# One filling block moved from RWKV's second inverse to the HGRN2 stage: half projections there in ten turns, four of them in turns 0 to 3

## The chip, the cores and the metric

The kernel runs on one NeuronCore of one Trainium2 chip. The metric is device time in microseconds (us) for one execution of the whole program, the median of three runs. The tensor engine (PE) multiplies; the vector engine (DVE), the scalar engine (ACT) and GpSimd (POOL) do elementwise work; SP issues most of the DMAs, and ACT and POOL issue some. Each engine takes its instructions in the order in which they were written down for it.

## The reference

One decoder layer over 1024 tokens of width 1024, in fp32. Three groups of heads share one input projection, and a feed-forward block and an embedding gate follow:

```python
z = rmsnorm(h, norm_mix_g) @ w_in            # (1024 x 1024) @ (1024 x 3840)
a_q, a_f, a_i, a_g, b_q, b_k, b_v, c_in = split(z)
o_a = hgrn2_mix(a_q, a_f, a_i, a_g, ...)     # 4 heads, gated linear recurrence
o_b = dilated_window_mix(b_q, b_k, b_v)      # 4 heads, three dilated windows
o_c = rwkv7_mix(c_in, ...)                   # 4 heads, delta rule recurrence
h = h + concat([o_a, o_b, o_c]) @ w_out
h = h + conv_glu_ffn(rmsnorm(h), ...)
h = h + sigmoid(rmsnorm(h) @ w_gate) * (p @ w_p)
return rmsnorm(h)
```

## The kernel before

`w_in` is cut into 30 blocks of 128 output columns, numbered 0 to 29. A block's projection is 8 row tiles times 2 token halves times 3 products: each operand is split into a rounded part and a remainder (`whi`, `wlo`, `xh`, `xl`), and `mm3` multiplies hi by hi (line 130), hi by lo (132) and lo by hi (134). That makes 48 matmuls of 128x512 for a block and 24 for one half of it. Blocks 0 to 7 feed RWKV directly. The other 22 (8 to 23 for HGRN2: f, q, i, g of each head; 24 to 29 for attention: q, k, v of two head pairs) are finished (scaled by the norm factor `R`; a sigmoid on f, q and g; q and g multiplied by the input of the sigmoid as well) and stored in DRAM as `z8` to `z29`, and are read back (`zl`) by the stage that uses them. Since PE needs none of RWKV's results for these products, they serve as filling.

`rwkv` treats two pairs of heads, p = 0 and 1, each in four steps. `rwkv_prep` makes the scores and projects one filling block. `rwkv_inverse` inverts unit triangular 32x32 blocks with 62 short DVE instructions (lines 698 and 700), turns the result through DRAM (`Tz`, `Uz`, then `Tc`) and needs no PE; meanwhile `project_rest` puts whole blocks on PE. `rwkv_main` goes through four groups of chunks (`rwkv_groups`), with PE, DVE, ACT and POOL in the order written; `fill` puts three matmuls of a further block between its steps, and `pending("z")` finishes a block at the start of the next group. The rest of those blocks follows with the output norm. The list `FILL` holds the number of blocks for each of these places, and the order of the blocks is fixed:

```python
js = iter((*range(8, 16), 24, 25, 26, 16, 17, 18, 20, 21, 22, 27, 28, 29, 19, 23))
...
self.project_rest([next(js) for _ in range(self.FILL[2 * p] - 1)])
...
steps = self.project_steps([next(js) for _ in range(self.FILL[2 * p + 1])])
...
self.rest = list(js)
```

Whatever is left then is projected in the HGRN2 stage, one half per turn, by `project_late` (tile `zp`). That stage interleaves four streams by an order that is written out for 38 turns: A (heads 0 and 2 of HGRN2), B (heads 1 and 3, from turn 6), C (attention, in the turns of `TURNS`) and F (a half projection, in the turns of `LATE`; its last turn only opens the tiles for the output projection):

```python
for r in range(38):
    order += "C" * (r in self.TURNS) + "A" + "B" * (r > 5) + "F" * (r in self.LATE)
interleave(order, {"A": A, "B": B, "C": self.swa(sp), "F": self.project_late(self.rest)})
```

A head of HGRN2 loads f and q (lines 987 to 992), multiplies the first scores (line 1008, `hsc`), then takes seven levels, one a turn: scores on PE (line 1029), a masked copy (1031) and two updates (1032, 1034) on DVE or POOL. In attention `swq` are scores (1186), 1193 their maximum on DVE, 1195 the exponential on ACT, `swt` transposes (1209) and `swo` values (1222). In this stage a scheduler may move an instruction of one stream past those of another on the same engine; in the four groups of `rwkv_main` it may only bring in work from outside.

Of the kernel before, what the change touches and what calls it, by code (L numbers as in the profile page):

```python
# [67 lines left out]
def interleave(order, streams):  # L68

    live = dict(streams)  # L70
    while live:
        for s in order:
            if s in live and next(live[s], STOP) is STOP:
                del live[s]
# [5 lines left out]
class Trunk:  # L80
# [227 lines left out]
    def phase_mix(self):  # L308
# [8 lines left out]
        with self.pool("hg") as slots, self.pool("sw") as sp:  # L317
# [8 lines left out]
            for r in range(38):  # L326
                order += "C" * (r in self.TURNS) + "A" + "B" * (r > 5) + "F" * (r in self.LATE)
            interleave(order, {"A": A, "B": B, "C": self.swa(sp), "F": self.project_late(self.rest)})

    TURNS = [i * 33 // 22 for i in range(23)]  # L330
    LATE = 0, 1, 4, 7, 9, 11, 13, 15, 17

    def mix_norm(self):

# [182 lines left out]
    def rwkv(self):  # L517
# [7 lines left out]
        for p in (0, 1):  # L525
            d = {}
            with tc.tile_pool(name=f"pre{p}", bufs=1) as tp:
                with tc.manual_schedule(engines={mybir.EngineType.PE}):
                    self.rwkv_prep(p, tp, lt, d, next(js))
                self.rwkv_inverse(p, tp, d)  # L530
            self.project_rest([next(js) for _ in range(self.FILL[2 * p] - 1)])
            E = mybir.EngineType
            self.pend = {}
            steps = self.project_steps([next(js) for _ in range(self.FILL[2 * p + 1])])
            with self.pool(f"rk{p}") as rp:
# [10 lines left out]
            self.rwkv_norm_out(p, sg, d, 1)  # L546
        self.rest = list(js)

    FILL = (6, 3, 6, 3)

    def rwkv_prep(self, p, tp, lt, d, j):

# [1343 lines left out]
```

## Time and profile before

| | |
|---|---|
| median of 3 runs | 1459.96 us (1458.23 to 1460.84) |
| the profiled execution, its own time | 1458.02 us |
| its span, first to last instruction | 1456.2 us |
| granted PE clock, mean of the span | 0.995 |
| PE busy | 1427.3 us, 98% |
| DVE busy | 1102.3 us, 76% |
| ACT busy | 635.3 us, 44% |
| second inverse, with the filling on PE | about 279 to 334 us |
| four groups of the second head pair | about 334 to 404 us |
| HGRN2 and attention stage | about 413 to 617 us |

A row of the timeline reads: start, duration, engine, line, operation, tiles written and read, shape, count; in brackets the time that the engine sat idle just before it and what ended that. A busy PE is one with a matmul in flight: neighbouring matmuls overlap, so that 48 rows of 0.39 us each take 10.9 us together. A row of a table by windows reads: window, its length, then busy time and number of instructions of PE, of PE's weight loads, of DVE, ACT and POOL, then granted clock, DMA share and GB/s.

### The profile page before, as it was taken

The page shows a single profiled execution, that of the slowest core. Times are in us where ns is not written, and L with a number is a line of the kernel's source. Part 1 is how long each engine was busy: PE and PEld are TensorE (multiplying, and loading weights), DVE is VectorE, ACT ScalarE, POOL GpSimd, SP SyncE. Part 2 cuts the span into 40 slices and gives each one's busy share as a digit, 9 for nine tenths or more (in the row PEclk, how much of TensorE's full clock was granted, in tenths as well). Part 3 has the DMA queues.
Part 4 walks back from the last instruction along what each step waited for, and adds up shares of the span by engine and source line. Part 5 has one row for each costly group of instructions (what it writes and reads, how often), then busy time and mean ns, then how long its engine had stood idle before and what let it go on. Part 6 is the DMA issues. An engine that isn't in the chain of part 4 may idle for free.

```text
span 1456.2 us, 20345 instructions
## 1 busy us (share of the span) xinstructions
PE 1427.3 (98%) x7480; PEld 1174.8 (81%) x7480; DVE 1102.3 (76%) x1672; ACT 635.3 (44%) x1131; POOL 447.3 (31%) x364
## 2 busy tenths in 40 slices
PE   9999999999999999899999999999999999999996
PEld 7888887888877777788878888888888888888885
DVE  6567565684677689637798889888888799777685
ACT  6531443213434565335544434444444444455552
POOL 2332342223421132222145545544454000002342
PEclk9999999999999999999999999999999999999998
DMA  5224021240151320165423332333333883352443
GB/s 215 69 82 114 30 74 58 66 129 31 58 203 44 116 73 23 66 224 209 153 93 109 109 100 96 109 103 107 108 96 122 311 287 96 103 165 58 127 157 115
DMA packets 80019, 167.84 MB, mean 115 GB/s; under 512 B 20080, under 2 KB 22256, under 8 KB 79920
## 3 DMA queue, kind: packets, MB, share of 16 engines
q1 hardware_dynamic: 65568, 145.44, 30.2%
q10 hardware_dynamic: 13408, 17.57, 3.6%
q0 software_dynamic: 944, 3.54, 0.7%
q8 instruction: 59, 0.97, 0.3%
q14 instruction: 40, 0.33, 0.1%
HBM read 120.12 MB, written 46.40 MB: 114 GB/s over the span
## 4 chain that ended last, share of the span: by engine, by line
PE 85%; DVE 6%; issue 3%; ACT 2%; POOL 2%; DMA 2%; SPq 0%; DVEq 0%; ACTq 0%; POOLq 0%
PE bg L1351 15%; PE bv L1351 11%; PE dp L130 8%; PE dp L134 8%; PE dp L132 8%; PE bg L1669 7%; PE bv L1669 7%; PE hsc L1029 2%; PE bv L130 1%; PE bv L134 1%; PE bv L132 1%; PE bg L130 1%; PE bg L132 1%; PE bg L134 1%; PE swq L1186 1%
## 5 line engine op out<-in xcount | busy, mean ns | idle before, releaser
L130 PE MATMUL dp<-xh,whi 128*128 128x512 f32 x544 | 197.5, 408 | 1.3 <-ACT xh L375 1.3
L134 PE MATMUL dp<-xh,wlo 128*128 128x512 f32 x544 | 189.1, 393 | 0.1
L132 PE MATMUL dp<-xl,whi 128*128 128x512 f32 x544 | 188.5, 392 | 0.4 <-DVE xl L376 0.3
L108 POOL TENSOR_TENSOR wlo<-raw,whi 128x512 fp32r<-128x512 f32 x84 | 136.4, 1643 | 75.1 <-ACT whi L106 75.1
L108 POOL TENSOR_TENSOR wlo<-wraw,whi 128x512 fp32r<-128x512 f32 x63 | 89.3, 1422 | 226.8 <-ACT whi L106 208.2
L1351 PE MATMUL bg<-t,whi 128*128 128x512 f32 x352 | 132.5, 389 | 0.8 <-DVE ct L1554 0.8
L106 ACT CAST whi<-wraw 128x512 fp32r<-128x512 f32 x120 | 72.6, 617 | 129.8 <-PE dp L132 87.0
L130 PEld LDWEIGHTS dp<-xh,whi 128*128 128x128 f32 x544 | 101.6, 189 | 24.0 <-issue 3.5
L134 PEld LDWEIGHTS dp<-xh,wlo 128*128 128x128 f32 x544 | 102.3, 188 | 22.3 <-POOL wlo L108 0.5
L132 PEld LDWEIGHTS dp<-xl,whi 128*128 128x128 f32 x544 | 102.4, 189 | 20.4 <-DVE xl L376 0.6
L108 POOL TENSOR_TENSOR wlo<-s,whi 128x512 fp32r<-128x512 f32 x44 | 66.6, 1514 | 160.9 <-ACT whi L106 160.9
L1669 PE MATMUL bg<-t,whi 128*128 128x512 f32 x308 | 94.9, 389 | 0.0
L1669 PE MATMUL bv<-t,whi 128*128 128x512 f32 x308 | 94.8, 389 | 0.0
L106 ACT CAST whi<-s 128x512 fp32r<-128x512 f32 x66 | 39.0, 620 | 122.3 <-PE bg L1351 113.4
L106 ACT CAST whi<-raw 128x512 fp32r<-128x512 f32 x88 | 52.7, 619 | 90.9 <-issue 48.3
L175 POOL TENSOR_TENSOR rst<-rst,mhalf 128x4 f32<-128x4 f32 (+1 forms) x9 | 10.1, 1130 | 222.7 <-DVE rst L173 222.7
L108 DVE TENSOR_TENSOR wlo<-wraw,whi 128x512 fp32r<-128x512 f32 x57 | 47.7, 836 | 40.2 <-ACT whi L106 35.8
L1351 PEld LDWEIGHTS bg<-t,whi 128*128 128x128 f32 x352 | 66.0, 188 | 14.7 <-ACT whi L106 1.1
L1665 ACT CAST t<-t 128x512 fp32r<-128x512 f32 x77 | 47.8, 623 | 47.6 <-PE bv L1669 34.1
L1669 PEld LDWEIGHTS bv<-t,whi 128*128 128x128 f32 x308 | 57.8, 188 | 12.0
L1669 PEld LDWEIGHTS bg<-t,whi 128*128 128x128 f32 x308 | 57.7, 188 | 12.0
L1351 PE MATMUL bg<-t,wlo 128*128 128x512 f32 x176 | 67.2, 389 | 0.0
(424 smaller groups left out, 3610.6 us busy)
## 6 DMA issues: line engine op xcount, KB each, us to landing
raw<-in_ffn_up_dram SPq DMA_DIRECT2D x44, 512.0 KB, 3.7
wraw<-in_w_in_dram SPq DMA_DIRECT2D x29, 512.0 KB, 3.7
z<-zst SPq DMA_DIRECT2D x18, 512.0 KB, 2.8
gb<-ct SPq DMA_DIRECT2D x33, 256.0 KB, 2.3
t<-gb SPq DMA_DIRECT2D x33, 256.0 KB, 2.8
t<-gt SPq DMA_DIRECT2D x33, 256.0 KB, 2.7
zl<-z SPq DMA_DIRECT2D x16, 512.0 KB, 4.1
wraw<-in_ple_gate_dram SPq DMA_DIRECT2D x16, 512.0 KB, 3.6
```

The costliest lines, as they stand in the source:

```text
L106: nc.scalar.copy(hi, src)
L108: eng.tensor_tensor(lo, src, hi.bitcast(F32), ALU.subtract)
L130: nc.tensor.matmul(ps[hf], wh, xh[hf], start=first, stop=False)
L132: nc.tensor.matmul(ps[hf], wh, xl[hf], start=False, stop=False)
L134: nc.tensor.matmul(ps[hf], wl, xh[hf], start=False, stop=last)
L175: nc.gpsimd.tensor_tensor(r2[:, :n], r[:, :n], self.mhalf[:, :n], ALU.pow)
L1029: nc.tensor.matmul(sc[:, c, :], ks[:, c * P:(c + 1) * P], view(qt, c * P, [2 * n, 64 // n], [HT + n, 2], [1, n]), start=True, stop=True)
L1186: nc.tensor.matmul(pq[h][:, b:b + w], d["q"][hs, qb * P:nk], d["k"][hs, b:b + w], start=True, stop=True)
L1351: nc.tensor.matmul(ps, w[part == 2][:, s], X[k][part == 1], start=start and k == part == 0, stop=k == 3 and part == 2, skip_group_check=no ...
L1665: nc.scalar.copy(xh, x)
L1669: nc.tensor.matmul(ps[m], wt[part == 2][:, m * P:(m + 1) * P], (xh, xl)[part == 1], start=k == part == 0, stop=k == NK - 1 and part == 2)
```

## The change

```diff
-    LATE = 0, 1, 4, 7, 9, 11, 13, 15, 17
+    LATE = 0, 1, 2, 3, 5, 7, 9, 11, 13, 15, 17
...
-    FILL = (6, 3, 6, 3)
+    FILL = (6, 3, 5, 3)
```

During the second inverse PE now has four whole blocks (26, 16, 17, 18) behind the one of `rwkv_prep` (25). Block 20 goes to the steps of `rwkv_main`, so that these hold 20, 21, 22 and no longer 21, 22, 27. Block 27 goes to the HGRN2 stage, which projects five blocks (27, 28, 29, 19, 23) in ten halves and no longer four in eight. The turns of the halves are 0, 1, 2, 3, 5, 7, 9, 11, 13, 15, where they were 0, 1, 4, 7, 9, 11, 13, 15.

On PE, between the inverse's filling and the first group of the second pair: the end of the filling and the start of the group (`dp` are the projections, `pt` transposes, `py` the first product with the inverse `T`). Before, the last block `dp_2787` (block 20) stands between `dp_2723` (block 18) and the group; of its 48 rows the last six are shown:

```order
L130 MATMUL dp_2787<-xh_119,whi_2783 128x512
L130 MATMUL dp_2787<-xh_103,whi_2783 128x512
L132 MATMUL dp_2787<-xl_120,whi_2783 128x512
L132 MATMUL dp_2787<-xl_104,whi_2783 128x512
L134 MATMUL dp_2787<-xh_119,wlo_2785 128x512
L134 MATMUL dp_2787<-xh_103,wlo_2785 128x512
L821 MATMUL pt_2891<-cst,v_2304 128x128 x2
L130 MATMUL dp_2894<-xh_105,whi_2845 128x512
L132 MATMUL dp_2894<-xl_106,whi_2845 128x512
L134 MATMUL dp_2894<-xh_105,wlo_2847 128x512
L860 MATMUL py_2901<-T_2885,ABt_2877 128x128 x4
```

```order
L132 MATMUL dp_2723<-xl_120,whi_2719 128x512
L132 MATMUL dp_2723<-xl_104,whi_2719 128x512
L134 MATMUL dp_2723<-xh_119,wlo_2721 128x512
L134 MATMUL dp_2723<-xh_103,wlo_2721 128x512
L821 MATMUL pt_2825<-cst,v_2304 128x128 x2
L130 MATMUL dp_2828<-xh_105,whi_2779 128x512
L132 MATMUL dp_2828<-xl_106,whi_2779 128x512
L134 MATMUL dp_2828<-xh_105,wlo_2781 128x512
L860 MATMUL py_2835<-T_2819,ABt_2811 128x128 x4
```

The group follows block 18 at once, and its first filling matmuls are those of block 20.

On DVE, from the end of the third group of the second pair through most of the fourth (`S` are steps of the state, `wlo` a weight's remainder, `X` a copy that the next PE product `pgm` reads). Before:

```order
L940 SCALAR_TENSOR_TENSOR S_3391<-pS_3392,gC_2414,N_3355 128x64
L940 SCALAR_TENSOR_TENSOR S_3398<-pS_3399,gC_2414,N_3355 128x64
L108 TENSOR_TENSOR wlo_3683<-wraw_3675,whi_3681 128x512
L940 SCALAR_TENSOR_TENSOR S_3405<-pS_3406,gC_2414,N_3355 128x64
L794 TENSOR_TENSOR U_3412<-Tc_2510,cst 128x512
L740 TENSOR_TENSOR sc_2307<-sc_2307,gnr_3303 128x512
L785 TENSOR_TENSOR AKt_3449<-sc_3444,pm_2858 128x256
L785 TENSOR_TENSOR W_2865<-sc_3444,pm_2858 64x4x64 x2
L108 TENSOR_TENSOR wlo_3857<-wraw_3853,whi_3855 128x512
L883 COPY_PREDICATED U_3412<-cmask,pu_3456 128x512
L828 COPY pb_2862<-pt_3462 64x2x64 x4
L470 TENSOR_TENSOR zst_3600<-dp_3183,rstd 128x512 x2
```

After:

```order
L108 TENSOR_TENSOR wlo_3616<-wraw_3612,whi_3614 128x512
L940 SCALAR_TENSOR_TENSOR S_3330<-pS_3331,gC_2414,N_3287 128x64
L940 SCALAR_TENSOR_TENSOR S_3337<-pS_3338,gC_2414,N_3287 128x64
L794 TENSOR_TENSOR U_3344<-Tc_2510,cst 128x512
L740 TENSOR_TENSOR sc_2307<-sc_2307,gnr_3235 128x512
L785 TENSOR_TENSOR AKt_3381<-sc_3376,pm_2792 128x256
L785 TENSOR_TENSOR W_2799<-sc_3376,pm_2792 64x4x64 x2
L883 COPY_PREDICATED U_3344<-cmask,pu_3388 128x512
L828 COPY pb_2796<-pt_3394 64x2x64 x4
L306 TENSOR_TENSOR dp_3117<-dp_3117,rstd 128x512
L108 TENSOR_TENSOR wlo_3733<-wraw_3725,whi_3731 128x512
L475 TENSOR_TENSOR zst_3532<-zst_3532,dp_3117 128x512
```

A weight's remainder now stands ahead of the last two steps of the state, where it stood ahead of the last; and the block finished here is 21, a q block with a sigmoid, of which the first half's scaling (306) and product (475) stand ahead of the copy `X`, where two plain scalings (470) of block 22 stood.

On ACT, about turn 15 of the HGRN2 stage (`hV` and `hkt` are the transposed values and keys of head 1, which PE's `hkv` needs; `ob` is attention's output, cast for the output projection). Before:

```order
L473 ACTIVATE zst_4475<-zp_4563 128x512
L1053 COPY hV_4621<-vt_4622 128x512
L1053 COPY hV_4621<-vt_4628 128x512
L1059 COPY hkt_4634<-vt_4635 128x512
L1195 ACT_TABLE_LOAD
L1195 ACTIVATE lg_4607,sden_4602<-lg_4607,sden_4602 128x128
L1195 ACTIVATE lg_4610,sden_4602<-lg_4610,sden_4602 128x128
L1059 COPY hkt_4634<-vt_4641 128x512
L155 CAST xh_4689<-ob_3827 128x512
```

After:

```order
L473 ACTIVATE zst_4478<-zp_4566 128x512
L155 CAST xh_4692<-ob_3830 128x512
L1053 COPY hV_4624<-vt_4625 128x512
L1195 ACT_TABLE_LOAD
L1195 ACTIVATE lg_4610,sden_4605<-lg_4610,sden_4605 128x128
L1195 ACTIVATE lg_4613,sden_4605<-lg_4613,sden_4605 128x128
L1053 COPY hV_4624<-vt_4631 128x512
L1059 COPY hkt_4637<-vt_4638 128x512
L1059 COPY hkt_4637<-vt_4644 128x512
```

The cast of `ob` moved ahead of all four copies, and the table load and two exponentials ahead of three of them.

## The prediction

> **What bounds the kernel now.** I read the page's head first, then a table by windows cut at the stages, then the timeline around the three places that the change touches. Head and table:
>
> ```profile
> span 1456.2 us, 20345 instructions
> PE 1427.3 (98%) x7480; PEld 1174.8 (81%) x7480; DVE 1102.3 (76%) x1672; ACT 635.3 (44%) x1131; POOL 447.3 (31%) x364
> PE 85%; DVE 6%; issue 3%; ACT 2%; POOL 2%; DMA 2%; SPq 0%; DVEq 0%; ACTq 0%; POOLq 0%
> core 0: us, PE busy (x) PEld busy (x) DVE busy (x) ACT busy (x) POOL busy (x), PEclk, DMA share, GB/s
> 279.00:334.30 55.30, 55.30 (x243) 45.37 (x242) 37.79 (x90) 7.19 (x11) 10.97 (x13) 1.00 0.36 106
> 334.30:413.00 78.70, 76.71 (x593) 63.82 (x592) 46.46 (x103) 33.49 (x100) 30.81 (x37) 1.00 0.23 75
> 426.60:440.00 13.40, 13.16 (x79) 10.35 (x78) 13.06 (x30) 5.60 (x17) 4.02 (x5) 1.00 0.31 98
> 440.00:490.00 50.00, 49.76 (x331) 37.86 (x331) 32.55 (x65) 24.93 (x48) 7.91 (x7) 1.00 0.12 38
> 490.00:520.00 30.00, 28.22 (x236) 24.54 (x234) 24.98 (x39) 18.01 (x31) 7.38 (x8) 1.00 0.38 141
> 520.00:545.00 25.00, 22.65 (x169) 17.34 (x165) 20.32 (x51) 17.51 (x42) 9.63 (x8) 1.00 0.29 96
> 545.00:580.00 35.00, 32.78 (x268) 25.49 (x269) 33.61 (x67) 19.74 (x41) 7.58 (x7) 1.00 0.05 16
> 580.00:617.00 37.00, 33.20 (x276) 28.99 (x276) 24.12 (x43) 14.30 (x26) 9.35 (x8) 1.00 0.17 52
> ```
>
> The chain that ended last is 85% PE, and PE is in use for 98% of the span. So a matmul that is moved from one place where PE is full to another costs there what it saves here. Only PE's idle time can be won: 2.0 us in the four groups (78.70 less 76.71), 0.2 at 426 to 440 and 0.2 up to 490, but 1.8, 2.4, 2.2 and 3.8 us in the last four windows, where DVE is busy up to 96% (33.61 of 35). The change puts its products at 427 to 440, ahead of that idle time.
>
> **The change part by part.**
>
> *One block less behind the second inverse.* The first row is PE alone in the stretch of the last block (20), the others the two tiles of the inverse that DVE builds, and PE's first products of the group:
>
> ```profile
> 323.40:334.30 10.90, 10.90 (x49) 1.00 0.13 55
> 321.35 0.69 DVE L794 TENSOR_TENSOR T<-Tc,cst 128x512 f32<-128x512 f32 x1 [0.16 <-DMA Tc<-Tz]
> 323.73 0.69 DVE L794 TENSOR_TENSOR U<-Tc,cst 128x512 f32<-128x512 f32 x1 [1.68 <-DMA Tc<-Uz]
> 334.30 0.38 PE L821 MATMUL pt<-cst,v 128*128 128x128 f32 x2
> 335.21 1.05 PE L860 MATMUL py<-T,ABt 128*128 128x128 f32 x8
> 337.92 1.06 PE L882 MATMUL pu<-U,Y 128*128 128x128 f32 x8
> ```
>
> The block is 48 matmuls in 10.9 us, a step of 0.227. Without it `pt` comes at 323.4, `py` at 335.21 - 10.9 = 324.3 and `pu` at 327.0. `T` is ready at 322.04 and `U` at 324.42: margins of 2.3 and 2.6 us. What covered the inverse's last 10 us was the block taken away; what covers it now is block 18, and it just does. DVE's and ACT's share of the removed block can only help. So -10.9 us, with nothing given back; a margin used up would be the next thing to show.
>
> *Other blocks inside the four groups.* Block 20's two sigmoids no longer fall into group 0; at the start of group 2 block 20 (scaling, sigmoid) is finished in place of 21 (scaling, sigmoid, product); in group 3 it is 21 in place of 22 (one scaling a half).
>
> ```profile
> 336.79 0.60 ACT L473 ACTIVATE zst<-dp 128x512 f32<-128x512 f32 x1
> 339.68 0.44 PE L821 MATMUL pt<-cst,khat 128*128 128x128 f32 x2 [0.49 <-ACT xr L828]
> 356.24 0.44 PE L821 MATMUL pt<-cst,khat 128*128 128x128 f32 x2
> 370.10 0.69 DVE L475 TENSOR_TENSOR zst<-zst,dp 128x512 f32<-128x512 f32 x1 [0.92 <-ACT zst L473]
> 370.82 0.70 DVE L306 TENSOR_TENSOR dp<-dp,rstd 128x512 f32<-128x512 f32 x1
> 371.55 0.60 ACT L473 ACTIVATE zst<-dp 128x512 f32<-128x512 f32 x1 [1.49 <-DVE dp L306]
> 372.68 1.16 PE L882 MATMUL pu<-U,Y 128*128 128x128 f32 x8 [0.77 <-ACT Y L861]
> ```
>
> In group 0 the sigmoid at 336.79 holds up ACT's copies, and PE waits 0.49 us for `xr`; group 1, without a sigmoid, shows no wait at the same product (356.24). I take -0.4. In group 2 the chain is DVE's product (370.10), the second scaling, the second sigmoid, ACT's copy `Y`, PE's `pu`. Without the product the scaling comes 0.7 sooner, and so does `Y`: of the 0.77 us wait I take -0.65. Late next is `xr` at the product after it, which moves along, so nothing more is won.
>
> ```profile
> 385.52 0.28 DVE L940 SCALAR_TENSOR_TENSOR S<-pS,gC,N 128x64 f32<-128x64 f32 x1 [0.57 <-PE pS L939]
> 385.72 1.40 DVE L108 TENSOR_TENSOR wlo<-wraw,whi 128x512 fp32r<-128x512 f32 x1
> 384.08 4.18 POOL L108 TENSOR_TENSOR wlo<-wraw,whi 128x512 fp32r<-128x512 f32 x3
> 392.38 0.69 DVE L108 TENSOR_TENSOR wlo<-wraw,whi 128x512 fp32r<-128x512 f32 x1 [1.14 <-ACT whi L106]
> 395.12 1.29 DVE L470 TENSOR_TENSOR zst<-dp,rstd 128x512 f32<-128x512 f32 x2 [0.32 <-PE dp L134]
> 396.46 0.43 DVE L903 COPY X<-px 64x256 f32<-64x256 f32 x1
> 397.19 1.05 PE L909 MATMUL pgm<-pb,X 128*128 128x128 f32 x8
> ```
>
> At the end of group 2 a weight's remainder (line 108) stands one step of `S` sooner. Before, it came behind the third step, which the last product still needs; now it comes ahead of it, and PE alternates with DVE there (each step waits 0.57 for PE). If it takes 1.40 us as here, beside POOL's three of the same kind, the third step is 0.8 late (1.40 less 0.57); if 0.69, 0.1. I take +0.8, since the row of that very place is the nearer. The Trainium skill ("SBUF — State Buffer", "Who interferes with whom") says that a DVE instruction with two inputs in SBUF and a GpSimd instruction that reads SBUF shut each other out; the pair 1.40 and 0.69 agrees, and without that rule's effect the sum below would be 0.7 us lower.
>
> In group 3 the scaling of 21 can start at 395.12, when its matmuls are done; 0.69 later ACT's sigmoid (0.60) and beside it line 108 (0.69), then the product (0.68): `X` starts at about 397.2 and ends at 397.6, `pgm` comes at 397.65 and not at 397.19. +0.45. The second product falls between two later steps of `S`, whose next PE products are behind three filling matmuls: 0.
>
> *The HGRN2 stage.* Two halves more, one behind the first scores `hsc` (line 1008), one behind level 1.
>
> ```profile
> 413.90:419.70 5.80, 5.80 (x26) 1.00 0.63 182
> 421.10:426.60 5.50, 5.50 (x27) 1.00 0.89 325
> 421.72 0.81 DVE L987 TENSOR_SCALAR zl<-zl,olb,lb 128x1024 f32<-128x1024 f32 x1 [0.66 <-DMA zl<-z]
> 429.85 1.54 PE L1029 MATMUL hsc<-qt,ks 128*128 128x128 f32 x8 [0.23 <-DVE hS L1010]
> 433.20 1.20 PE L1029 MATMUL hsc<-qt,ks 128*128 128x128 f32 x8
> ```
>
> A half takes 5.5 us, 5.8 where it begins the stage. Two are +11.1. Against this, the waits of turns 2 and 3 have 5.5 us of matmuls in them now: the idle 0.23 goes, and the 0.34 by which level 1 is longer than level 2 (1.54 and 1.20). I take -0.5, between nothing and -1.0. DVE's and ACT's work for a half is the same as inside RWKV, and the loads of f and q (here at 421.72, 5 us ahead of PE's need at 426.6) stand behind the same weight load and the same two halves as before. The DMA queue of SP keeps its order there but for the block numbers; POOL's load for attention now stands behind one weight remainder, long before its turn. Nothing is queued that was not.
>
> *From turn 15 on* the program is the same, but the scheduler's order differs. The rows on which it acts:
>
> ```profile
> 525.96 0.56 ACT L1059 COPY hkt<-vt 128x512 f32<-128x512 f32 x1
> 540.67 1.13 PE L1029 MATMUL hsc<-qt,ks 128*128 128x128 f32 x8 [1.37 <-DVE qt L1034]
> 593.58 1.13 PE L1029 MATMUL hsc<-qt,ks 128*128 128x128 f32 x8 [2.11 <-DVE qt L1034]
> ```
>
> ACT's last copy for `hkv` ended at 526.52; now the cast (0.62) and a sigmoid's wait stand ahead of it, which makes it 1 to 2 us later, while DVE and PE do attention work sooner in exchange. DVE's total is unchanged and it is the fuller engine from 545 on, so I take 0, between -2.35 (all of PE's idle time at 520 to 545) and +2.
>
> *Sum:* -10.9 - 0.4 - 0.65 + 0.8 + 0.45 + 11.1 - 0.5 + 0 = -0.1 us. On the profiled execution's 1458.02 us (its span 1456.2 and 1.8 around it) this gives 1457.9; the median of the three runs is 1.94 above that execution, and against it the forecast is 1459.9 us: no change that can be measured. By 0.2% or 2.9 us I can tell a change from none here.
>
> **The rivals.**
>
> *Faster: early filling lets DVE run ahead.* PE has filling for 11.1 us more when DVE is at its fullest, 13.06 of 13.40 us at 426 to 440. If DVE comes out of it with a lead, the 1.8 and 2.4 us that PE idles at 490 to 545 shrink: at most 4.1 us, 1455.8. For it: PE's longest idle time there ends with DVE. Against it: from 440 to 490 DVE has only 32.55 us of work in 50 and is fed by PE, so a lead ends there. The Trainium skill ("Perfetto Trace Analysis", "Optimization Strategy") advises to interleave stretches that are bound by different engines; by it this rival would be the likeliest, but these rows show the filling added where PE itself is full.
>
> *Slower: ACT's new order at turn 15.* The later `hkt` delays `hkv` by up to 2 us, DVE's chain of head 1 behind it, and the wait of 1.37 us at 540.67 grows by as much again: about +3.6, 1463.5. It decides if those copies end more than 2 us later against the stage's start. For it: PE waits for this chain already, at 540.67 and again at 593.58. Against it: attention work taken sooner is work saved later.
>
> *Slower: the inverse shows.* If `T` or `U` is over 2.3 us later than here, each further us is one of span. Two late would be 1462. Against it: nothing is added ahead of them on any engine or queue.
>
> **How the numbers follow.** The forecast 0.53, faster 0.25, the first slower one 0.17, the second 0.05. The forecast's terms are small and of both signs, and its own range is 1458.0 to 1461.8 (the bounds of the copies and of the HGRN2 waits). The range over all, 1455.8 to 1463.5, reaches to both rivals' full price. Faster by over 0.2%: 0.27, the first rival and a little of the forecast's lower end; slower: 0.20; within: 0.53.
>
> **What would show it.** Right: the product `py` of the second pair's first group comes 10 to 11 us sooner with no wait for `T` or `U`; `pu` of group 2 waits under 0.3 us; a wait of about 0.8 us among the last steps of `S` of group 2; PE without idle time between the first scores and level 2; the stage's first products of the output projection within 2 us of where they are. Wrong: PE idle over 1 us ahead of `py` or `pu` (the inverse), or a total idle time of PE from 490 to 617 that differs from the 10.2 us here by more than 2.

## The result, and the profile after

The changed kernel takes 1463.96 us (median, 1461.76 to 1464.92) against 1459.05 us for the kernel before in the same comparison: a ratio of 1.0032, interval 1.0023 to 1.0041. It is slower by 0.32%, 4.9 us, where I forecast no change (1459.9) and a range that ended at 1463.5. The profiled execution took 1463.13 us, 5.11 more than that of before.

The page's head, its chain, and the table by windows of the changed kernel, cut at the same places of the program as before:

```profile
span 1461.4 us, 20346 instructions
PE 1430.2 (98%) x7480; PEld 1175.8 (80%) x7480; DVE 1107.3 (76%) x1673; ACT 636.5 (44%) x1131; POOL 445.4 (30%) x364
PE 86%; DVE 5%; issue 3%; ACT 3%; POOL 2%; DMA 1%; SPq 0%; DVEq 0%; ACTq 0%; POOLq 0%
core 0: us, PE busy (x) PEld busy (x) DVE busy (x) ACT busy (x) POOL busy (x), PEclk, DMA share, GB/s
323.40:401.90 78.50, 77.23 (x594) 63.83 (x593) 47.07 (x102) 33.58 (x100) 33.09 (x38) 1.00 0.22 75
438.70:488.70 50.00, 50.00 (x333) 38.65 (x333) 28.20 (x53) 23.12 (x43) 7.48 (x7) 1.00 0.08 27
488.70:518.70 30.00, 28.22 (x236) 24.53 (x234) 24.86 (x42) 18.02 (x31) 5.60 (x6) 1.00 0.39 141
518.70:543.70 25.00, 24.11 (x172) 18.33 (x169) 20.03 (x52) 17.89 (x44) 9.98 (x9) 1.00 0.31 96
543.70:578.70 35.00, 32.17 (x270) 25.12 (x270) 32.96 (x64) 19.77 (x40) 7.98 (x7) 1.00 0.05 16
578.70:615.40 36.70, 32.95 (x268) 29.22 (x267) 22.82 (x41) 13.91 (x26) 8.91 (x8) 0.95 0.13 44
```

In the stages that the change touches nothing is lost: PE idles 1.27 us in the four groups (2.0 before) and 9.25 us in the last four windows (10.2 before). PE busy has grown by 2.9 us with the same 7480 matmuls, and one window shows a granted clock of 0.95. So some matmuls became slower. Following the same PE products through both traces gives the account. The shift against before is -1.71 us at 590 us of the span, and everything after that is loss. PE's rows at which the shift changes, the changed kernel first, then the same sums in the kernel before:

```profile
591.87 1.48 PE L1029 MATMUL hsc<-qt,ks 128*128 128x128 f32 x8 [2.12 <-DVE qt L1034]
666.66 1.02 PE L167 MATMUL ps_ss<-few,acc 128*128 128x1 f32 x8 [1.19 <-DVE acc L201]
1377.32 1.05 PE L167 MATMUL bv<-few,acc 128*128 128x1 f32 x8 [1.60 <-DVE acc L201]
1405.44 0.50 PE L132 MATMUL bv<-xh,whi 128*128 128x512 f32 x1 [0.40 <-POOL xh L157]
```

```profile
666.29 1.02 PE L167 MATMUL ps_ss<-few,acc 128*128 128x1 f32 x8 [0.27 <-DVE acc L201]
1373.28 1.05 PE L167 MATMUL bv<-few,acc 128*128 128x1 f32 x8
```

And two windows of the changed kernel that follow the first two of these waits at once:

```profile
592.50:595.90 3.40, 3.40 (x29) 3.18 (x29) 1.30 (x2) 0.00 (x0) 0.00 (x0) 0.50 0.02 5
667.60:671.00 3.40, 3.40 (x9) 2.70 (x9) 3.17 (x6) 2.70 (x5) 1.38 (x1) 0.50 0.79 323
```

The sum: -1.7 at 590; +1.6 for the window at half clock at 592.5; +0.5 for the longer wait at 666; +2.0 for the window at 667.6 and the rows behind it; +1.6 for the wait at 1377; +0.6 at 1405; +0.5 from there to the end. That is +5.1. The last three waits stand in the output projection and the embedding gate, hundreds of microseconds behind the moved block. That the sum of this one execution comes so near to the 4.9 us of the medians is in part luck: the window at 592.5 comes in some executions and not in others. e5 and e9 below are the same program up to there, and their profiles do not have it.

What reaches so far is a counter. A weight block is split into `whi` and `wlo` in two halves, and which engine computes a half's remainder (line 108) goes by the parity of the number of names given so far:

```python
self.uid += 1
parts.append(self.split2(raw[:, b * HT:(b + 1) * HT],
                         eng or (self.nc.gpsimd if self.uid % 2 else self.nc.vector)))
```

A block that is projected whole takes two names (`dp`, `zst`), one in the HGRN2 stage three (`zst` and two `zp`). With one block moved, POOL and DVE change places in every later block that is split this way, and the scheduler orders DVE, ACT and POOL anew around that. In the embedding gate this gives, on DVE and then on POOL, before:

```profile
1366.58 2.24 DVE L201 TENSOR_TENSOR acc<-acc,sqt 128x512 f32<-128x512 f32 x2 [0.27 <-ACT sqt L200]
1368.73 0.68 DVE L108 TENSOR_TENSOR wlo<-wraw,whi 128x512 fp32r<-128x512 f32 x1
1369.33 1.48 DVE L201 TENSOR_TENSOR acc<-acc,sqt 128x512 f32<-128x512 f32 x2
1366.10 1.36 POOL L108 TENSOR_TENSOR wlo<-wraw,whi 128x512 fp32r<-128x512 f32 x1 [4.87 <-ACT whi L106]
1373.93 1.65 POOL L108 TENSOR_TENSOR wlo<-wraw,whi 128x512 fp32r<-128x512 f32 x1 [6.47 <-ACT whi L106]
```

and after:

```profile
1367.99 1.29 DVE L201 TENSOR_TENSOR acc<-acc,sqt 128x512 f32<-128x512 f32 x2 [0.70 <-ACT sqt L200]
1369.80 3.98 DVE L201 TENSOR_TENSOR acc<-acc,sqt 128x512 f32<-128x512 f32 x4
1375.50 2.36 DVE L201 TENSOR_TENSOR acc<-acc,sqt 128x512 f32<-128x512 f32 x2
1370.63 1.81 POOL L108 TENSOR_TENSOR wlo<-wraw,whi 128x512 fp32r<-128x512 f32 x1 [4.61 <-ACT whi L106]
1375.03 1.68 POOL L108 TENSOR_TENSOR wlo<-wraw,whi 128x512 fp32r<-128x512 f32 x1 [2.60 <-ACT whi L106]
```

Two sums alone take 1.29 us. Before, one remainder on POOL falls beside them and the next comes only after the sums that PE waits for. Now two fall beside them: four sums take 3.98 us and the pair with the last sum 2.36. Taken one by one, the sum beside the first remainder takes 1.60 us and the one beside the second 1.76, where a sum alone takes 0.69. The eight sums up to the one that PE waits for now take 9.3 us (1367.99 to 1377.26), where they took 8.2 (1365.02 to 1373.22); the other 0.5 of the 1.60 us is their later start. The Trainium skill ("SBUF — State Buffer", "Who interferes with whom") has DVE instructions with two inputs in SBUF and GpSimd instructions that read SBUF shut each other out; these times agree.

### The profile page after: what moved, and what is told of

Same layout as the page of the kernel before. It is cut to its first block, busy times and chain, and to the rows that moved or that the text cites. A ratio compares the mean times of both kernels' runs of the same rounds, so it can differ in the third digit from the quotient of the medians.

```text
span 1461.4 us, 20346 instructions
## 1 busy us (share of the span) xinstructions
PE 1430.2 (98%) x7480; PEld 1175.8 (80%) x7480; DVE 1107.3 (76%) x1673; ACT 636.5 (44%) x1131; POOL 445.4 (30%) x364
## 4 chain that ended last, share of the span: by engine, by line
PE 86%; DVE 5%; issue 3%; ACT 3%; POOL 2%; DMA 1%; SPq 0%; DVEq 0%; ACTq 0%; POOLq 0%
PE bg L1351 15%; PE bv L1351 11%; PE dp L130 8%; PE dp L134 7%; PE dp L132 7%; PE bg L1669 7%; PE bv L1669 7%; PE hsc L1029 2%; PE zp L130 1%; PE swq L1186 1%; PE zp L132 1%; PE zp L134 1%; PE swo L1222 1%; PE swt L1209 1%; PE bv L132 1%
## 5 line engine op out<-in xcount | busy, mean ns | idle before, releaser
L130 PE MATMUL dp<-xh,whi 128*128 128x512 f32 x528 | 192.8, 409 | 1.2 <-ACT xh L375 1.2
L134 PE MATMUL dp<-xh,wlo 128*128 128x512 f32 x528 | 184.4, 393 | 1.1 <-POOL wlo L108 1.1
L132 PE MATMUL dp<-xl,whi 128*128 128x512 f32 x528 | 184.0, 392 | 0.3 <-DVE xl L376 0.3
L175 POOL TENSOR_TENSOR rst<-rst,mhalf 128x4 f32<-128x4 f32 (+1 forms) x9 | 10.2, 1132 | 225.2 <-DVE rst L173 225.2
```

The costliest lines, as they stand in the source:

```text
L130: nc.tensor.matmul(ps[hf], wh, xh[hf], start=first, stop=False)
L132: nc.tensor.matmul(ps[hf], wh, xl[hf], start=False, stop=False)
L134: nc.tensor.matmul(ps[hf], wl, xh[hf], start=False, stop=last)
```

## The experiments

Theory A: the loss is the turned alternation in the later phases. Theory B: it belongs to the moved block. Theory C: the windows at half clock are all of it.

**The counter alone.** e1 is the changed kernel, e2 the kernel before, each with one name more behind the stage:

```diff
-            interleave(order, {...})
+            interleave(order, {...}); self.uid += 1
```

> The change, with the counter of names raised by one after the HGRN2 stage, so that the weights' remainders of all later phases go to POOL and DVE in the order that the kernel before has; up to the end of the HGRN2 stage it is the changed kernel. Theory A (the loss is the alternation of POOL and DVE, turned over in the later phases by one name more): the waits of 0.5, 1.6 and 0.6 us for DVE in the output projection and in the embedding gate go, and the gain of 1.3 to 1.7 us at 590 us of the span stays: 1457.4 to 1459.3 us, the upper end if a half-speed window of the clock (1.7 us) stays at 592 us. Theory B (the loss belongs to the moved block itself, wherever it shows): as the changed kernel, 1463 to 1465 us. Theory C (the two half-speed windows of the clock are the whole loss, the alternation has no part): 1460.5 to 1462 us if one of them goes, 1464 if none does.

> The kernel before with the counter raised by one after the HGRN2 stage and nothing else: POOL and DVE change places for the weights' remainders of all later phases. Theory A: slower by the waits that the changed kernel shows there, 0.5 + 1.6 + 0.6 = 2.7 us, and by 1.9 more if the longer wait ahead of the sums of the output projection brings a half-speed window with it: 1461.5 to 1464 us. Theory B: no change, 1458.5 to 1459.6 us. Theory C: no change unless a half-speed window appears, and then 1.7 us for each.

e1: 1458.88 us, ratio to before 0.9992 (0.9984 to 1.0001). e2: 1462.78, ratio 1.0029 (1.0017 to 1.0041). The change without the turned alternation is not slower; the turned alternation without the change is slower by as much as the changed kernel. B falls, A holds. e2's profile has the changed kernel's wait at the sums, and a window of the clock behind it:

```profile
1375.44 1.05 PE L167 MATMUL bv<-few,acc 128*128 128x1 f32 x8 [1.60 <-DVE acc L201]
1376.50:1380.00 3.50, 3.50 (x9) 2.73 (x10) 2.11 (x5) 0.63 (x2) 1.44 (x1) 0.51 0.65 213
```

In e1 PE's products run 1.19 us ahead of before from 455 us to the wait at 592: that is the moved block's own gain. A window at half clock behind that wait, in its profiled execution, takes 1.6 us back.

**Where the alternation costs.** e6 raises the counter only at the embedding gate, so that the output projection keeps the turned order.

```diff
     def phase_ple(self, ple):
-        nc = self.nc
+        nc = self.nc; self.uid += 1
```

> The changed kernel, where the counter is raised by one only at the start of the embedding gate: the output projection keeps the turned alternation, the embedding gate has that of the kernel before. Theory A, with the loss split by place: the waits of 1.6 and 0.56 us in the embedding gate go, and the half-speed window that they bring in some executions: 1461.0 to 1461.8 us, so half of what raising it after the HGRN2 stage gives (1458.9). If the output projection is where it all begins: 1463 to 1464.

1459.05 us, ratio 1.0000 (0.9991 to 1.0008). I expected half of the effect and got all of it: by the medians the embedding gate carries the 4.9 us. The intervals, over 1 us to either side, leave room for a part in the output projection: e6's profile still has the wait there (1.11 us) and a window at half clock behind it (at 666.87), which together cost that execution 2.4 us. How often they come is not shown; the mean granted clock over e6's 11 executions, 0.9947, is that of e1's (0.9948). The sums of the embedding gate do not wait now:

```profile
1374.26 1.05 PE L167 MATMUL bv<-few,acc 128*128 128x1 f32 x8
```

**The wait itself.** e5 keeps the turned alternation and lets PE come to these sums six matmuls later; e10 does the same to the kernel before.

```diff
-        hooks = {(0, 4): {0: lambda: sums("n"), 4: lambda: spread("n")},
+        hooks = {(0, 4): {2: lambda: sums("n"), 6: lambda: spread("n")},
```

> The changed kernel, where in the embedding gate PE's sums (line 167, which wait 1.60 us for DVE's acc at 1377.32) come two row tiles later in PE's own order, that is 6 matmuls of 0.227 us, and the spread of the factor (line 181) two later as well. If the turned alternation costs by this wait (theory A): the wait shrinks from 1.60 to about 0.2, 1462.3 to 1462.8 us. If the wait only moves on to the spread, because POOL's power (1.45 us) comes later too: 1463.5 to 1464.5 us.

> Control for e5: the kernel before with the same two hooks two row tiles later. It has no wait at those sums, so moving them gives nothing by itself: 1458.9 to 1459.8 us. If moving them were a gain of its own (of e5's 2.9 us): 1456.5 to 1458.

e5: 1461.03 us, ratio 1.0010 (1.0001 to 1.0019), 2.9 us below the changed kernel. e10: 1459.57, ratio 1.0001 (0.9992 to 1.0009), so the later place gains nothing by itself. In e5 the wait has shrunk by 1.33 us, and by the shift of the products behind the sums the kernel wins 1.3 there:

```profile
1377.33 1.05 PE L167 MATMUL bv<-few,acc 128*128 128x1 f32 x8 [0.27 <-DVE acc L201]
```

The time fell by about twice that, more than I expected. The other half would be the window at half clock that such a wait brings in some executions, which the next run tests. The granted clocks of all executions fit that: their mean is 0.9933 in the changed kernel (7 executions) and 0.9941 in e5 (11), and 0.0008 of 1460 us is 1.2 us. This is an estimate, since single executions differ by 0.002 and more.

**PE kept in use during the waits.** e9 is the changed kernel with transposes of the unit matrix ahead of both sums (10 and 14); the core of the edit:

```diff
             bank[n] = self.banks("v")
+            for c in range(14 * (n == "n")):
+                nc.tensor.transpose(bank[n][:, HT + c % 4 * P:HT + (c % 4 + 1) * P], self.ident, self.ident)
             r[n] = self.rstd_sums(accs[n], 1.0 / 1024, EPS, bank[n][:, 0:4])
```

> The changed kernel with matmuls of no use put on PE into its two later waits, so that the waits stay as long as they are and only PE is not idle in them: 10 transposes of the unit matrix ahead of the output projection's sums (wait 1.19 us at 666.66) and 14 ahead of the embedding gate's (1.60 us at 1377.32). If these waits cost twice, once by themselves and once by a half-speed window of PE's clock after them (about 1.7 us in an execution where it comes): the windows at 667 and 1377 are gone and the time falls by 1 to 3 us, to 1461 to 1463. If the windows have nothing to do with PE's idle time there, or cost nothing: 1463.5 to 1464.5.

```profile
665.13 1.02 PE L167 MATMUL ps_ss<-few,acc 128*128 128x1 f32 x8 [1.27 <-DVE acc L201]
1373.50 1.69 PE L1747 MATMUL bv<-cst 128*128 128x128 f32 x14
1375.28 1.05 PE L167 MATMUL bv<-few,acc 128*128 128x1 f32 x8
1376.00:1381.00 5.00, 5.00 (x26) 4.12 (x27) 3.08 (x6) 1.14 (x2) 1.01 (x1) 1.00 0.52 161
```

1462.60 us, ratio 1.0024 (1.0016 to 1.0033), 1.4 us below the changed kernel, whose interval it overlaps. The wait in the embedding gate is filled and is as long as it was. The clock behind it is 1.00, but so it is in the profile of the changed kernel, so this row alone shows nothing. The transposes of the output projection ran too early: they filled nothing and cost 1.0 us themselves (from 662.37 to 663.38). The mean granted clock of an execution is 0.995 or 0.996 in 9 of 12 here, and 0.992 to 0.994 in 6 of 7 of the changed kernel; the means, 0.9949 and 0.9933, differ by 0.0016, an estimated 2.3 us, and less the 1.0 that is near the 1.4 measured. The direction is as expected; by the intervals the size of the window's share is not settled. Theory C falls with e2, where the alternation alone costs 3.3 us, and with e5, whose profile has two windows at half clock (at 494 and 668) as the changed kernel's has and is 1.5 us shorter.

**The turns of the halves.** e3 changes the turns of the kernel before; e4 is the changed kernel with e1's line and the two halves more at the end.

```diff
-    LATE = 0, 1, 4, 7, 9, 11, 13, 15, 17
+    LATE = 0, 1, 2, 3, 5, 7, 9, 11, 13
```

```diff
-    LATE = 0, 1, 2, 3, 5, 7, 9, 11, 13, 15, 17
+    LATE = 0, 1, 4, 7, 9, 11, 13, 15, 17, 19, 21
```

> FILL as before (6, 3, 6, 3), so that the block stays behind the second inverse, and only the turns of the eight halves changed, to 0, 1, 2, 3, 5, 7, 9, 11: the same products, two of the halves sooner and the last at turn 11. The alternation of later phases is that of the kernel before. If early filling gives DVE a lead (my first rival): 1455 to 1457.5 us. If filling is worth the same wherever PE is full, but the idle time at 490 to 545 us loses the halves of turns 13 and 15 that lay beside it: slower by 0 to 3 us, 1459 to 1462.

> The change with its ten halves at turns 0, 1, 4, 7, 9, 11, 13, 15, 17, 19 (the two more come last and not in turns 2 and 3), and with the alternation of the kernel before in the later phases. If PE's idle time of 490 to 617 us (10.2 us) is what filling can win, the two late halves (11 us) fill part of it: 1453 to 1457 us. If there DVE (busy 96% at 545 to 580) only moves back by the halves' own DVE work, 1457 to 1460 us.

e3: 1462.94 us, ratio 1.0021 (1.0013 to 1.0030), a little above the second expectation. It also takes two late halves away, so by itself it does not settle my first rival, early filling that gives DVE a lead. e1 does: with four halves in turns 0 to 3 its PE idles 1.78, 2.34 and 2.21 us at 490 to 520, 520 to 545 and 545 to 580, and before it was 1.78, 2.35 and 2.22. That rival falls. e4: 1467.72, ratio 1.0055 (1.0044 to 1.0067), slower than either expectation. A row of e3, then a row and a window of e4:

```profile
517.23 2.05 PE L1029 MATMUL hsc<-qt,ks 128*128 128x128 f32 x8 [2.12 <-DVE qt L1034]
```

```profile
550.36 0.90 PE L1209 MATMUL swt<-cst,lg 128*128 128x128 f32 x3 [5.29 <-DVE hS L1031]
545.00:580.00 35.00, 28.85 (x197) 21.37 (x197) 29.57 (x55) 21.04 (x41) 10.00 (x8) 0.80 0.13 38
```

Late halves do not win where DVE sets the pace: PE waits 5.29 us for one masked copy, and 13.6 us at half clock begin within that wait, at 546.7. Ahead of that copy (549.59) DVE does one scaling of a half (0.69 us), but mostly HGRN2's own work: an output scaling (line 1114, 1.76 us) and the set-up of the next head (lines 987 to 992, 6.1 us from 542.97), between whose instructions the kernel before puts its masked copies. That the later halves made the scheduler choose this order is likely, but no run shows it by itself, and how much of e4's loss is DVE and how much the clock was not separated.

**A better version.** PE's longest wait in both e1 and the kernel before, 2.1 us at 592, is for `qt`. e7 is e1 with `qt` updated ahead of the masked copy in each level, e8 the kernel before with the same exchange.

```diff
-            nc.vector.copy_predicated(S3[0], mask(l), sc)
             ...
             nc.vector.tensor_tensor(qq, qq, view(Tc, 1, [nb - 1, 2], [2, nb // 2], [0, n]), ALU.mult)
+            nc.vector.copy_predicated(S3[0], mask(l), sc)
```

> The kernel of e1 (the change, later phases as before), with the two DVE instructions of each HGRN2 level exchanged: the update of the queries (0.67 us), for which PE's next level waits, ahead of the masked copy (0.73 us), for which nothing waits before the output. If PE's waits of 1.37 and 2.11 us at 540 and 592 us end with this chain on DVE: each is 0.6 to 0.7 shorter, with others of the stage 1 to 3 us less, and the wait at 592 then no longer fills over half of a window of the clock, so that its half-speed window (1.6 us) goes: 1455 to 1457.5 us. If DVE's total work is the bound there: 1458 to 1459.5.

> The kernel before with the same exchange on DVE, as the control for e7: if the gain comes from PE's waits of 1.37 and 2.11 us, which both kernels have, 1.5 to 3 us less than before, 1456 to 1457.5; the half-speed window at 592 shows in fewer of its executions, so it wins less than e7 against e1. If not, 1459 to 1460.

e7: 1457.74 us, ratio 0.9991 (0.9982 to 0.9999), the fastest and the only one whose interval lies below 1. e8: 1458.01, ratio 0.9993 (0.9984 to 1.0002). PE's wait, in e1 and in e7:

```profile
592.39 2.00 PE L1029 MATMUL hsc<-qt,ks 128*128 128x128 f32 x8 [2.11 <-DVE qt L1034]
```

```profile
592.11 1.16 PE L1029 MATMUL hsc<-qt,ks 128*128 128x128 f32 x8 [1.66 <-DVE qt L1031]
```

In e7 the eight products take 1.16 us, in e1 2.00, at half clock. Both times lie a little above what I expected for a gain: the wait at 592 fell by 0.45 us and not by 0.6 to 0.7, and another, at 551, grew from 0.35 to 1.09. Nor did e8 win less than e7, as I had thought it would. The exchange gives about 1.1 us on e1 and 1.5 on before; the moved block, with the alternation kept, gives 0.3 (e7 against e8) to 0.6 (e1 against before), neither of which these intervals tell from nothing.

## Why the prediction was wrong

- *One block less behind the inverse*, -10.9: measured -10.92 at `py`, without a wait. `T` and `U` even came 1.6 and 3.1 us sooner than before:

```profile
319.78 0.69 DVE L794 TENSOR_TENSOR T<-Tc,cst 128x512 f32<-128x512 f32 x1 [0.18 <-DMA Tc<-Tz]
320.66 0.69 DVE L794 TENSOR_TENSOR U<-Tc,cst 128x512 f32<-128x512 f32 x1 [0.19 <-DMA Tc<-Uz]
324.30 1.05 PE L860 MATMUL py<-T,ABt 128*128 128x128 f32 x8
```

- *Group 0*, -0.4: measured -0.45. *Group 2*, -0.65: -0.71. *Group 3*, +0.45: +0.50. The rows of group 3 run as I chained them, product, then `X`, then `pgm`:

```profile
384.73 0.69 DVE L475 TENSOR_TENSOR zst<-zst,dp 128x512 f32<-128x512 f32 x1
385.45 0.43 DVE L903 COPY X<-px 64x256 f32<-64x256 f32 x1
385.93 1.16 PE L909 MATMUL pgm<-pb,X 128*128 128x128 f32 x8 [0.34 <-DVE X L903]
```

- *End of group 2*, +0.8: measured +0.32. The remainder took 1.08 us and not the 1.40 of the nearest row, with POOL's three beside it as foreseen:

```profile
372.81 1.08 DVE L108 TENSOR_TENSOR wlo<-wraw,whi 128x512 fp32r<-128x512 f32 x1
```

- *The HGRN2 stage*, +10.6: measured +9.8 (the shift goes from -11.14 at the first scores to -1.32). The filled waits, to which I had allowed 1.0 at most, gave 1.3.
- *From turn 15 on*, 0: measured -0.4 up to 590 us. ACT's new order did delay head 1's `hkv` by 1.8 us against the levels around it, as my slower rival had it, but PE's wait of 1.37 us behind it went away instead of growing:

```profile
539.91 1.13 PE L1029 MATMUL hsc<-qt,ks 128*128 128x128 f32 x8
```

  And the new order was not the block's: e1 has ACT's old order there, e2 the new one. The counter made it, through a later weight that is split already in this stage: before, POOL computes its first remainder (at 517.61) and DVE the second (520.65), and so in e1; in the changed kernel DVE comes first (517.59) and then POOL (519.79).

The shift that all these terms leave at 590 us is -1.7 us and not -0.1 (as rounded here they add up to -1.9). Were that all, the forecast would have held, and none of the signs of being wrong that I had listed came; they all looked at the stages that the change touches. The forecast's own range, 1458.0 to 1461.8, was narrower than the bounds that it names, which add up to 1457.0 to 1462.4; that decided nothing here. The step that failed is *"From turn 15 on the program is the same, but the scheduler's order differs"*: I priced that at the three rows about turn 15, and everything behind the stage at nothing without saying so. The order of the later phases differed as well, and that cost the 4.9 us, by the medians in the embedding gate (e6): a wait of PE of 1.60 us for one sum, 0.6 more for a later one, and for about 2 us windows at half clock. The last is an estimate, from the mean granted clocks of 0.9933 in the changed kernel and 0.9947 in e6 (0.0014 of 1460 us). The remaining 0.7 us stays open. DVE's total unchanged, on which I rested the 0, is no bound on a wait for one sum. No rival of mine was this one, and the granted clock, 1.00 in every window that I quoted, had no term.

## What to carry to other kernels

Compare the order of the whole program, not of the stage that was edited: a counter, a pool's turn or a scheduler's cost can carry an edit to places where nothing was meant to change, and undoing that alone (one line here) tells a change from its side effect. Where engines alternate, choose by the block's own index, so that an edit elsewhere can't turn the choice over. A matmul that waits in PE's fixed order for the last of a chain of short sums is worth a place some matmuls later; its wait can cost twice.

## What the runs showed of the hardware

PE drops to half clock for 3.413 us after much shorter waits than I would have thought, in windows that run on a grid of their own: in e4 they begin at 485.23, 546.67 and 604.70 us, 18 and 17 steps of 3.413 us apart. Over the twelve profiles, in steps of that grid from 14 to 1435 us of the span: of the steps in which PE idled 1.97 us or more, 7 of 7 were followed by one at half clock (one of them, in e4, was at half clock itself); with 1.06 to 1.8 us, 6 of about 45; with less, none but inside e4's long stretch. The kernel before waits 2.11 us at 593.58 too, but in its profile the wait lies across two steps (0.84 and 1.26 us) and no half clock follows; in e1 it lies in one, and it does. Such a window costs 1.6 us behind 592 (0.11% of this kernel) and 2.0 behind 667, and executions of one program differ by it: the changed kernel, e5 and e9 are the same up to 592, and of their profiles only the first has the window there. The Trainium skill ("TensorE: Matmul & The Clock Gate", "What's actually happening") gives a free-running window of 3413 ns and half clock after an idle window; the length agrees, but here 2 us of idle time in a window are enough.
